# Differential attention on one core: the second softmax's factor in an accumulating form and a tile later, the head norm's statistics on GpSimd

## The chip, the core and the metric

The kernel runs on one core of a Trainium2 chip. The metric is the time of one execution on the device, in microseconds (us). A core has five engines that run side by side and meet at semaphores: TensorE (PE in the rows; its weight loads are PEld), VectorE (DVE), ScalarE (ACT), GpSimd (POOL) and SyncE (SP), which issues the DMAs here. Each engine takes its instructions in the order of its own queue. SBUF is the working memory, PSUM is where TensorE writes.

## What is computed

The program is a two-layer trunk over 1024 latent tokens and 256 context tokens, width 1024. The change lies in the mixer of the second layer, differential attention with 8 heads. Each head has two softmaxes over all 1280 keys, and the second is subtracted with a weight `lam`:

```python
def diff_attn_core(q, k, v, lam):
    s = jnp.einsum('bqhcd,bkhcd->bhcqk', q, k) * DIFF_HEAD_DIM ** -0.5
    p = jax.nn.softmax(s, axis=-1)
    w = p[:, :, 0] - lam * p[:, :, 1]
    return jnp.einsum('bhqk,bkhe->bqhe', w, v)

def finish(o):                       # o: (b, l, 8 heads, 128)
    o = rms_norm(o, subln_gain) * (1.0 - lam_init)
    return o.reshape(b, l, D_MODEL) @ w_out
```

`rms_norm` divides each row of 128 by the root of its mean square plus EPS. A common factor of a row cancels in it, apart from EPS, so the kernel never divides by the first softmax's sum.

## The kernel before

The attention stage works in 16 groups, one for each head `h` and half `qg` of the queries (512 rows). A group has four query tiles `j` of 128 rows, and each tile two units, `c` = 0 and 1, one for each softmax: 128 units in all.

A unit (`unit` in `qk_units`) writes the scores of 128 queries against 1280 keys to PSUM by TensorE (`sc` 1024 wide, `ct` 256 wide). VectorE copies them to SBUF negated and takes the row minimum on the way, with an accumulator output (L1017 and L1018, in the rows TENSOR_SCALAR_CACHE_REDUCE, each followed by a short DVE_READ_ACCUMULATOR). ScalarE takes the exponential and the row sum (L1019). After the second unit of a tile the two exponentials are combined: VectorE forms the factor -lam * sum0 / sum1, 128 rows by 1 column, with a reciprocal (L1022) and a `scalar_tensor_tensor` (L1023); then e1 is multiplied by it, on GpSimd for `j` in `POOLM` = (1, 2, 3) (L1029) and on ScalarE for `j` = 0 (L1031); then GpSimd adds it to e0 (L1032). In the very first group two tiles are combined by VectorE alone (`RAMP`, L1025).

The main loop goes over the groups and over ten blocks `kt` of 128 keys. For each block TensorE transposes the four combined tiles (L1187), ScalarE and VectorE split the result in a high and a low part (`split`, L55 and L56, tile `wt`), and TensorE multiplies with the values in three passes (L1191 to L1193, into `po`). `advance` keeps the units up to five ahead of the next group, so the scores of later groups are made in between. There are 2 PSUM buffers for `sc`, 3 buffers for e1 and 11 for e0.

After a group `post` runs: ScalarE copies `po` out, TensorE transposes it back (L1051), VectorE copies it (L1053), ScalarE sums squares (L1056), VectorE squares the sums of the first softmax for the EPS term (L1059). Once a head has both halves, `norm` adds the two terms (L1067) and takes an inverse root by three Newton steps in `rsqrt_ops` (L60, L62, and three times L65, L67, L69): twelve VectorE instructions on 128 rows by 8 columns for a head. GpSimd multiplies with the result (L1071). For the last head `norm` runs for each half by itself, and the multiplication is VectorE's.

Each engine's order is fixed when the program is built.

Of the kernel before, what the change touches and what calls it, by code (L numbers as in the profile page):

```python
# [13 lines left out]
I32 = mybir.dt.int32  # L14
AF = mybir.ActivationFunctionType
ALU = mybir.AluOpType
# [4 lines left out]
P = 128  # L21
# [4 lines left out]
T = L + LC  # L26
# [4 lines left out]
EPS = 1e-6  # L31
LAM_INIT = 0.8 - 0.6 * math.exp(-0.3)
# [3 lines left out]
def trunk(tc, a, dbg=None, stop=99):  # L36
    nc = tc.nc
    V, S, G, PE = nc.vector, nc.scalar, nc.gpsimd, nc.tensor
# [7 lines left out]
    def r32(ap):  # L46
        return ap.bitcast(F32)
# [10 lines left out]
    def rsqrt_ops(y, v, t, steps=3):  # L58
        yi = y.bitcast(I32)
        V.tensor_scalar(yi, v.bitcast(I32), 1, None, op0=ALU.logical_shift_right)  # L60
        yield
        V.tensor_scalar(yi, yi, -1, 0x5F3759DF, op0=ALU.mult, op1=ALU.add)  # L62
        yield
        for _ in range(steps):
            V.tensor_tensor(out=t, in0=y, in1=y, op=ALU.mult)  # L65
            yield
            V.scalar_tensor_tensor(out=t, in0=t, scalar=-0.5, in1=v, op0=ALU.mult, op1=ALU.mult)  # L67
            yield
            V.scalar_tensor_tensor(out=y, in0=t, scalar=1.5, in1=y, op0=ALU.add, op1=ALU.mult)  # L69
            yield  # L70

    def run(*gens):

        gens = list(gens)
        while gens:
            for g in list(gens):
                try:
                    next(g)
                except StopIteration:
                    gens.remove(g)  # L80

    def rsqrt(y, v, t):
        run(rsqrt_ops(y, v, t))
# [3 lines left out]
    def later(n, fn):  # L87
        pend.append([n, fn])
# [85 lines left out]
    for n, i in enumerate(PAIRS):  # L174
# [4 lines left out]
        if n % 2:  # L179
            j = n // 2  # L180
# [21 lines left out]
    subln = vec[:, 152:153]  # L202
# [234 lines left out]
    for dq in range(4):  # L437
        for i in range(2):
# [5 lines left out]
                                   op0=ALU.mult, op1=ALU.subtract)  # L444
# [406 lines left out]
    for j in range(2):  # L851
        for s in range(2):
            for cc in range(2):
                V.tensor_tensor(out=tabs[:, j, s, :, cc * HD:(cc + 1) * HD], in0=rope[s],
                                in1=gns[:, j, cc * HD:(cc + 1) * HD].unsqueeze(1).broadcast_to([P, 8, HD]), op=ALU.mult)
# [62 lines left out]
    def load_k(h):  # L918
        heads[h] = [[kq.tile([P, T], F32R, name=f"k{c}") for c in range(2)]]
        for c in range(2):  # L920
            nc.sync.dma_start(r32(heads[h][0][c]), kD[2 * h + c])
# [25 lines left out]
    op = up3.enter_context(tc.tile_pool(name="op", bufs=1, reuse_waits="tile"))  # L947
# [24 lines left out]
    nlam = cst.tile([P, 1], F32, name="nlam")  # L972
    V.tensor_tensor(out=nlam, in0=ls[:, 3:4], in1=ls[:, 2:3], op=ALU.subtract)
    V.tensor_scalar(nlam, nlam, -LAM_INIT, None, op0=ALU.add)
    sg = cst.tile([P, 1], F32, name="sg")
    V.tensor_scalar(sg, subln, 1.0 - LAM_INIT, None, op0=ALU.mult)

    oT = {}
    pairs = {}
    NE, LEAD, POOLM, RAMP = (11, 3), 5, (1, 2, 3), (1, 3)  # L980

    def load_v(h):
        vs = ap.tile([P, 2, 10, P], F32R, name="v")
        for s in range(2):
            nc.sync.dma_start(r32(vs[:, s]), vD[s, :, h * P:(h + 1) * P].rearrange("(t p) e -> p t e", p=P))
        heads[h].append(vs)

    def qk_units(h, qg):

        if (h, qg) not in queries:  # L990
            if qg == 0:
                load_k(h)
            load_q(h, qg)
        if qg == 0:
            load_v(h)
        ks, qs = heads[h][0], queries[h, qg]
        st = ap.tile([P, 16, 4], F32, name="st", bufs=6)
        wts = [None] * 4
        es_ = {}
        ct = {}  # L1000

        def scores(out, c, jsl, ksl):
            PE.matmul(out, qs[:, c, 0, jsl], ks[c][:, ksl], start=True, stop=False)
            PE.matmul(out, qs[:, c, 1, jsl], ks[c][:, ksl], start=False, stop=True)  # L1004

        def unit(j, c):
            jsl = slice(j * P, (j + 1) * P)
            col = lambda i: st[:, i, j:j + 1]
            sc = pss.tile([P, 2, 512], F32, name="sc")
            for bk in range(2):  # L1010
                scores(sc[:, bk], c, jsl, slice(bk * 512, (bk + 1) * 512))
            if c == 0:
                ct[j] = pst.tile([P, 2, LC], F32, name="ct", bufs=1)
                for cc in range(2):
                    scores(ct[j][:, cc], cc, jsl, slice(L, T))
            e = ap.tile([P, T], F32, name=f"e{c}", bufs=NE[c])
            V.tensor_scalar(e[:, 0:L], sc.rearrange("p a b -> p (a b)"), -1.0, 3.0e38, op0=ALU.mult, op1=ALU.min, accum_out=col(c))  # L1017
            V.tensor_scalar(e[:, L:T], ct[j][:, c], -1.0, col(c), op0=ALU.mult, op1=ALU.min, accum_out=col(4 + c))  # L1018
            S.activation(out=e, in_=e, func=AF.Exp, scale=-1.0, bias=col(4 + c), accum_out=col(10 + c))  # L1019
            es_[c] = e  # L1020
            if c == 1:
                V.reciprocal(col(12), col(11))  # L1022
                V.scalar_tensor_tensor(out=col(12), in0=col(12), scalar=nlam, in1=col(10), op0=ALU.mult, op1=ALU.mult)  # L1023
                if (h, qg) == (0, 0) and j in RAMP:
                    V.scalar_tensor_tensor(out=es_[0], in0=es_[1], scalar=col(12), in1=es_[0], op0=ALU.mult, op1=ALU.add)  # L1025
                    wts[j] = es_[0]
                    return
                if j in POOLM:
                    G.tensor_tensor(out=es_[1], in0=es_[1], in1=col(12).broadcast_to([P, T]), op=ALU.mult)  # L1029
                else:  # L1030
                    S.activation(out=es_[1], in_=es_[1], func=AF.Copy, scale=col(12))  # L1031
                G.tensor_tensor(out=es_[0], in0=es_[0], in1=es_[1], op=ALU.add)  # L1032
                wts[j] = es_[0]

        return [lambda j=j, c=c: unit(j, c) for j in range(4) for c in range(2)], st, wts

# [2 lines left out]
    def post(h, qg, po, st):  # L1039

        both = h < H - 1
        if qg == 0:
            posts[h] = (ap.tile([P, 4, 8], F32, name="sn"), {})
        sn, ons = posts[h]
        of = ap.tile([P, 512], F32, name="of", bufs=1)
        S.activation(out=of, in_=po, func=AF.Copy)

        def p1():
            pt = pst.tile([P, 512], F32, name="pt")
            for j in range(4):  # L1050
                PE.transpose(out=pt[:, j * P:(j + 1) * P], in_=of[:, j * P:(j + 1) * P], identity=ident)  # L1051
            on = ap.tile([P, 512], F32, name="on", bufs=2)
            V.tensor_copy(on, pt)  # L1053
            for j in range(4):
                jk = ap.tile([P, P], BF16, name="jk")
                S.activation(out=jk, in_=pt[:, j * P:(j + 1) * P], func=AF.Square, accum_out=sn[:, 0, 4 * qg + j:4 * qg + j + 1])  # L1056
            ons[qg] = on
            z = sn[:, 1, 4 * qg:4 * qg + 4]
            V.scalar_tensor_tensor(out=z, in0=st[:, 10], scalar=EPS, in1=st[:, 10], op0=ALU.mult, op1=ALU.mult)  # L1059
            if not both:  # L1060
                norm((qg,))
            elif qg:
                later(1, lambda: norm((0, 1)))

        def norm(qs):
            s0, s1, s2_, s3 = (sn[:, i, 4 * qs[0]:4 * qs[-1] + 4] for i in range(4))
            V.scalar_tensor_tensor(out=s0, in0=s0, scalar=1.0 / P, in1=s1, op0=ALU.mult, op1=ALU.add)  # L1067
            rsqrt(s2_, s0, s3)
            for q in qs:
                on = ons[q]  # L1070
                (G if both else V).tensor_tensor(out=on.rearrange("p (j d) -> p j d", j=4), in0=on.rearrange("p (j d) -> p j d", j=4),  # L1071
                                                 in1=sn[:, 2, 4 * q:4 * q + 4].unsqueeze(2).broadcast_to([P, 4, P]), op=ALU.mult)
                later(6 + 2 * q if both else 2, lambda q=q, on=on: p2(q, on))

        def p2(q, on):
            pt = pst.tile([P, 512], F32, name="pt")
            for j in range(4):
                PE.transpose(out=pt[:, j * P:(j + 1) * P], in_=on[:, j * P:(j + 1) * P], identity=ident)
            if h % 2 == 0:
                pairs[q] = ot(h + q, F32)  # L1080
            oT[q, h] = pairs[q][:, h % 2]
            S.activation(out=oT[q, h], in_=pt, func=AF.Copy, scale=sg)

        later(2 if both else 1, p1)
# [14 lines left out]
    def advance(target):  # L1099
        nonlocal done  # L1100
        while done < target:
            if not stream:
                n = len(info)
                if n >= len(groups):
                    return
                need(n)
            stream.pop(0)()
            done += 1
# [68 lines left out]
    op0 = oproj0()  # L1177
    L0, LS = 3, 5
    advance(8 + L0)
    for gi, (h, qg) in enumerate(groups):  # L1180
        st, wts = info[gi]
# [376 lines left out]
    out = a["out"].rearrange("o t d -> (o t) d")  # L1558
# [124 lines left out]
```

## Time and profile before

| | us |
|---|---|
| median of 3 runs | 2795.05 (2791.34 to 2796.46) |
| the profiled execution | 2793.9 |
| its span, first to last instruction | 2792.1 |
| stretch of the 128 attention units in it, 1538.6 to 1948.0 | 409.4 |

The page of the profile gives the busy time of each engine over the span. A stretch of it is read from the busy times of that window, the instructions grouped by line, and the instructions in order of time. A group of instructions has a count, a busy time and a mean; one line gives the shortest, median and longest of them.

### The profile page before, as it was taken

What the parts mean: (1) busy time and instruction counts of PE and PEld (TensorE: products, weight loads), DVE (VectorE), ACT (ScalarE), POOL (GpSimd) and SP (SyncE); (2) the same over time, 40 slices, a digit from 0 to 9 for tenths busy, and PEclk for the clock granted to TensorE, in tenths of its full rate; (3) what the DMA queues carried; (4) which work ended last, traced back from release to release, by engine and by line L of the source; (5) the groups of instructions that cost most, each with busy time, mean ns of one, the idle gap of its engine ahead of it and who ended that gap; (6) DMA issues with size and microseconds to landing.
All of it is one profiled execution on the core that took longest, in us unless ns stands there. A gap on an engine that the chain in (4) does not pass through costs nothing.

```text
span 2792.1 us, 35671 instructions
## 1 busy us (share of the span) xinstructions
PE 2664.8 (95%) x13234; PEld 2182.4 (78%) x13234; DVE 1609.0 (58%) x2920; ACT 1106.5 (40%) x1940; POOL 960.1 (34%) x648
## 2 busy tenths in 40 slices
PE   6999999999999999999999888898987999999999
PEld 4678888888888888878888666676766788888887
DVE  7744644434333434586764999999666555555342
ACT  5642333222322111333343776687434333334231
POOL 4431024221211000013351676777046666651000
PEclk9999999999999999999999999999999999999999
DMA  6682122222222111143335523222243222226352
GB/s 210 203 272 84 31 76 80 84 87 79 88 83 68 39 38 38 50 138 116 114 114 185 157 83 107 83 69 84 80 128 94 87 87 82 82 79 208 109 181 87
DMA packets 284480, 290.64 MB, mean 104 GB/s; under 512 B 16249, under 2 KB 201874, under 8 KB 284306
## 3 DMA queue, kind: packets, MB, share of 16 engines
q1 hardware_dynamic: 282146, 284.69, 32.8%
q0 software_dynamic: 2160, 3.67, 0.4%
q8 instruction: 104, 1.70, 0.3%
q14 instruction: 70, 0.57, 0.1%
HBM read 234.83 MB, written 53.48 MB: 103 GB/s over the span
## 4 chain that ended last, share of the span: by engine, by line
PE 71%; DVE 11%; issue 8%; POOL 6%; DMA 2%; ACT 2%; SPq 0%; POOLq 0%; DVEq 0%; ACTq 0%
PE ps L50 12%; PE ps L52 12%; PE ps L51 12%; PE b L1418 4%; PE b L1416 4%; PE b L1417 4%; PE b L51 3%; PE b L52 3%; PE b L50 3%; DVE e L1017 2%; POOL xn L894 2%; POOL t L895 2%; PE pt L1187 1%; PE ps L229 1%; DVE wt L56 1%
## 5 line engine op out<-in xcount | busy, mean ns | idle before, releaser
L50 PE MATMUL ps<-un,whl 128*128 128x512 f32 x1184 | 464.4, 393 | 1.4 <-ACT XT L592 1.2
L51 PE MATMUL ps<-un,whl 128*128 128x512 f32 x1184 | 461.3, 390 | 0.0
L52 PE MATMUL ps<-un,whl 128*128 128x512 f32 x1184 | 460.9, 389 | 0.0
L56 DVE TENSOR_TENSOR whl<-raw,whl 128x512 fp32r<-128x512 f32 x219 | 170.8, 793 | 271.2 <-ACT whl L55 270.5
L50 PEld LDWEIGHTS ps<-un,whl 128*128 128x128 f32 x1184 | 222.4, 188 | 54.9 <-issue 3.5
L52 PEld LDWEIGHTS ps<-un,whl 128*128 128x128 f32 x1184 | 222.3, 188 | 46.9
L51 PEld LDWEIGHTS ps<-un,whl 128*128 128x128 f32 x1184 | 222.6, 188 | 44.8 <-issue 0.7
L55 ACT ACTIVATE whl<-raw 128x512 fp32r<-128x512 f32 x219 | 134.7, 628 | 246.2 <-PE ps L52 178.1
L736 DVE SCALAR_TENSOR_TENSOR XT<-ps,mods,XT 128x512 f32<-128x512 f32 (+1 forms) x264 | 170.3, 660 | 85.2 <-PE ps L52 84.9
L262 POOL TENSOR_TENSOR acc<-acc,aw 128x512 f32<-128x512 f32 x84 | 112.6, 1340 | 296.4 <-ACT acc L258 231.2
L1032 POOL TENSOR_TENSOR e<-e,e 128x1280 f32<-128x1280 f32 x62 | 182.9, 2951 | 91.3 <-DMA q<-qD 52.8
L1019 ACT ACTIVATE e<-e,st 128x1280 f32<-128x1280 f32 x128 | 174.7, 1366 | 62.0 <-DVE e L1018 45.7
L607 POOL TENSOR_TENSOR nacc<-nacc,s 128x512 f32<-128x512 f32 (+1 forms) x35 | 41.0, 1172 | 414.2 <-ACT s L606 392.7
L51 PE MATMUL ps<-u,whl 128*128 128x256 f32 x592 | 167.5, 283 | 0.0
L52 PE MATMUL ps<-u,whl 128*128 128x256 f32 x592 | 167.4, 283 | 0.0
L50 PE MATMUL ps<-u,whl 128*128 128x256 f32 x592 | 167.3, 283 | 0.0
L1017 DVE TENSOR_SCALAR_CACHE_REDUCE e<-sc 128x1024 f32<-128x1024 f32 x128 | 154.8, 1216 | 10.3 <-PE sc L1004 8.1
L819 PE MATMUL ps<-whl,un 128*128 128x512 f32 x384 | 152.9, 398 | 0.0
L820 PE MATMUL ps<-whl,un 128*128 128x512 f32 x384 | 150.2, 392 | 1.0 <-DVE whl L56 0.9
L821 PE MATMUL ps<-whl,un 128*128 128x512 f32 x384 | 149.9, 391 | 0.0
L51 PE MATMUL b<-au,wu 128*128 128x512 f32 x336 | 130.9, 390 | 0.1
L50 PE MATMUL b<-au,wu 128*128 128x512 f32 x336 | 130.8, 390 | 0.0
(419 smaller groups left out, 6436.3 us busy)
## 6 DMA issues: line engine op xcount, KB each, us to landing
aw<-in_w_ada SPq DMA_DIRECT2D x96, 256.0 KB, 2.8
raw<-in_ffn_w_in SPq DMA_DIRECT2D x88, 256.0 KB, 2.9
wr<-in_ffn_w_out SPq DMA_DIRECT2D x42, 512.0 KB, 4.1
wada<-in_w_ada SPq DMA_DIRECT2D x48, 256.0 KB, 3.3
un<-in_w_ada SPq DMA_DIRECT2D x48, 256.0 KB, 4.5
raw<-in_diff_w_in SPq DMA_DIRECT2D x48, 256.0 KB, 3.5
rq<-in_ffn_w_in SPq DMA_DIRECT2D x24, 512.0 KB, 5.6
raw<-in_ffn_w_out SPq DMA_DIRECT2D x44, 256.0 KB, 2.9
```

Of the source, the lines that this page charges most:

```text
L50: PE.matmul(out, wh, mh, start=start, stop=False)
L51: PE.matmul(out, wh, ml, start=False, stop=False)
L52: PE.matmul(out, wl, mh, start=False, stop=stop)
L55: S.activation(out=hl[:, 0], in_=src, func=AF.Copy)
L56: (lo_eng or V).tensor_tensor(out=hl[:, 1], in0=src, in1=r32(hl[:, 0]), op=ALU.subtract)
L736: V.scalar_tensor_tensor(out=xs, in0=pt, scalar=gmod[c][:, nn:nn + 1], in1=xs, op0=ALU.mult, op1=ALU.add)
L819: PE.matmul(pt, hk[:, 0, tsl], ws[k][:, 0], start=k == 0, stop=False)
L820: PE.matmul(pt, hk[:, 0, tsl], ws[k][:, 1], start=False, stop=False)
L821: PE.matmul(pt, hk[:, 1, tsl], ws[k][:, 0], start=False, stop=k == NC - 1)
L1017: V.tensor_scalar(e[:, 0:L], sc.rearrange("p a b -> p (a b)"), -1.0, 3.0e38, op0=ALU.mult, op1=ALU.min, accum_out=col(c))
L1019: S.activation(out=e, in_=e, func=AF.Exp, scale=-1.0, bias=col(4 + c), accum_out=col(10 + c))
L1032: G.tensor_tensor(out=es_[0], in0=es_[0], in1=es_[1], op=ALU.add)
```

## The change

The factor's second step becomes a `tensor_scalar` with two column operands and an accumulator output, whose one-column sum is the factor; the multiplication and addition of a tile are written out after the next unit's exponential, through the list `comb`; `POOLM` becomes (0, 2), so GpSimd and ScalarE multiply in turn (14 of the 46 multiplications by GpSimd go to ScalarE); and the EPS term, the sum of the terms and the inverse root go to GpSimd, in a form that GpSimd has (`rsqrt_pool`, 14 instructions), except the inverse root of the last head's second half. The mean's 1/128 moves into the constants.

```diff
+    def rsqrt_pool(y, v, t, steps=3):
+        G.tensor_scalar(y.bitcast(I32), v.bitcast(I32), -0.5, float(0x5F3759DF), op0=ALU.mult, op1=ALU.add)
+        G.tensor_scalar(v, v, -0.5, None, op0=ALU.mult)
+        for _ in range(steps):
+            G.tensor_tensor(out=t, in0=y, in1=y, op=ALU.mult)
+            G.tensor_tensor(out=t, in0=t, in1=v, op=ALU.mult)
+            G.tensor_scalar(t, t, 1.5, None, op0=ALU.add)
+            G.tensor_tensor(out=y, in0=y, in1=t, op=ALU.mult)
...
-    V.tensor_scalar(sg, subln, 1.0 - LAM_INIT, None, op0=ALU.mult)
+    V.tensor_scalar(sg, subln, (1.0 - LAM_INIT) * math.sqrt(P), None, op0=ALU.mult)
...
-    NE, LEAD, POOLM, RAMP = (11, 3), 5, (1, 2, 3), (1, 3)
+    NE, LEAD, POOLM, RAMP = (11, 3), 5, (0, 2), (1, 3)
...
+            while comb:
+                comb.pop()()
             if c == 1:
-                V.reciprocal(col(12), col(11))
-                V.scalar_tensor_tensor(out=col(12), in0=col(12), scalar=nlam, in1=col(10), op0=ALU.mult, op1=ALU.mult)
...
+                e0, e1 = es_[0], es_[1]
+                wts[j] = e0
+                comb.append(lambda: combine(j, col, e0, e1))
+
+        def combine(j, col, e0, e1):
+
+            V.reciprocal(col(12), col(11))
+            V.tensor_scalar(col(13), col(12), col(10), nlam, op0=ALU.mult, op1=ALU.mult, accum_out=col(14))
...
+            if j in POOLM:
+                G.tensor_tensor(out=e1, in0=e1, in1=col(14).broadcast_to([P, T]), op=ALU.mult)
+            else:
+                S.activation(out=e1, in_=e1, func=AF.Copy, scale=col(14))
+            G.tensor_tensor(out=e0, in0=e0, in1=e1, op=ALU.add)
...
-            V.scalar_tensor_tensor(out=z, in0=st[:, 10], scalar=EPS, in1=st[:, 10], op0=ALU.mult, op1=ALU.mult)
+            G.tensor_tensor(out=z, in0=st[:, 10], in1=st[:, 10], op=ALU.mult)
...
-            V.scalar_tensor_tensor(out=s0, in0=s0, scalar=1.0 / P, in1=s1, op0=ALU.mult, op1=ALU.add)
-            rsqrt(s2_, s0, s3)
+            G.tensor_scalar(s1, s1, P * EPS, None, op0=ALU.mult)
+            G.tensor_tensor(out=s0, in0=s0, in1=s1, op=ALU.add)
+            (rsqrt if qs == (1,) else rsqrt_pool)(s2_, s0, s3)
```

How the queues change is seen at two places. On VectorE, in the third group, this stood before around two tiles' factors (names as in the code; a number after a name tells buffers apart):

```order
L1018 TENSOR_SCALAR e_13290,st<-ct,st 128x256
L56 TENSOR_TENSOR wt<-pt,wt 128x512
L1017 TENSOR_SCALAR e_13319,st<-sc 128x1024
L1022 RECIPROCAL st<-st 128x1
L1017 TENSOR_SCALAR e_13339,st<-sc 128x1024
L1023 SCALAR_TENSOR_TENSOR st<-st,nlam 128x1
L1018 TENSOR_SCALAR e_13319,st<-ct,st 128x256
```

and this stands there now (L1029 and L1030 are the unit's two copies, L1042 and L1043 the factor, in the changed file's numbering):

```order
L1030 TENSOR_SCALAR e_13290,st<-ct,st 128x256
L56 TENSOR_TENSOR wt<-pt,wt 128x512
L1029 TENSOR_SCALAR e_13315,st<-sc 128x1024
L1029 TENSOR_SCALAR e_13339,st<-sc 128x1024
L1030 TENSOR_SCALAR e_13315,st<-ct,st 128x256
L1042 RECIPROCAL st<-st 128x1
L56 TENSOR_TENSOR wt<-pt,wt 128x512
L1043 TENSOR_SCALAR st<-st,nlam 128x1
```

The factor of a tile has moved behind the next unit's copies, and its second step has changed its form.

On GpSimd, in the fourth group, where the first head's norm falls, this stood before:

```order
L1032 TENSOR_TENSOR e_13554<-e_13554,e_13574 128x1280
L1029 TENSOR_TENSOR e_13637<-e_13637,st 128x1280
L1032 TENSOR_TENSOR e_13603<-e_13603,e_13637 128x1280
L1029 TENSOR_TENSOR e_13704<-e_13704,st 128x1280
L1032 TENSOR_TENSOR e_13667<-e_13667,e_13704 128x1280
L1071 TENSOR_TENSOR on<-on,sn 128x512 x2
```

and now this (L1048 is the multiplication, L1051 the addition, L1077 to L1086 the statistics, L74 to L80 the inverse root):

```order
L1051 TENSOR_TENSOR e_13550<-e_13550,e_13574 128x1280
L1048 TENSOR_TENSOR e_13637<-e_13637,st 128x1280
L1077 TENSOR_TENSOR sn<-st 128x4
L1051 TENSOR_TENSOR e_13599<-e_13599,e_13637 128x1280
L1085 TENSOR_SCALAR sn<-sn 128x8
L1086 TENSOR_TENSOR sn<-sn 128x8
L74 TENSOR_SCALAR sn<-sn 128x8
L75 TENSOR_SCALAR sn<-sn 128x8
L77 TENSOR_TENSOR sn<-sn 128x8
L78 TENSOR_TENSOR sn<-sn 128x8
L79 TENSOR_SCALAR sn<-sn 128x8
L80 TENSOR_TENSOR sn<-sn 128x8
```

The norm's small instructions (eight more of the last four lines' kind follow) stand between the additions of the third and of the fourth tile of the group, and the fourth tile's multiplication has left this queue.

## Rows read from the trace of the kernel before

**Rows 1.** The page's busy us, share of the span and instructions of each engine.
```profile
PE 2664.8 (95%) x13234; PEld 2182.4 (78%) x13234; DVE 1609.0 (58%) x2920; ACT 1106.5 (40%) x1940; POOL 960.1 (34%) x648
```
**Rows 2.** Busy times by stretch: all units; eight with a norm; eight without one.
```profile
core 0: us, PE busy (x) PEld busy (x) DVE busy (x) ACT busy (x) POOL busy (x), PEclk, DMA share, GB/s
1538.60:1948.00 409.40, 357.56 (x1872) 279.42 (x1872) 388.70 (x887) 302.91 (x557) 295.43 (x118) 0.97 0.34 97
1621.00:1653.20 32.20, 25.18 (x129) 19.29 (x127) 30.40 (x64) 21.83 (x42) 22.46 (x11) 0.95 0.40 114
1653.20:1675.80 22.60, 21.92 (x121) 17.28 (x121) 20.88 (x52) 18.34 (x40) 17.50 (x7) 1.00 0.20 54
```
**Rows 3.** VectorE by line from 1538 to 1948: count, busy us and mean ns, idle before.
```profile
L56 DVE TENSOR_TENSOR wt<-pt,wt 128x512 fp32r<-128x512 f32 x142 | 95.4, 683 | 2.7 <-ACT wt L55 2.3
...
L1023 DVE SCALAR_TENSOR_TENSOR st<-st,nlam 128x1 f32<-128x1 f32 x63 | 37.1, 589 | 0.1
...
L1067 DVE SCALAR_TENSOR_TENSOR sn<-sn 128x8 f32<-128x8 f32 x6 | 8.1, 1358 | 0.2 <-ACT jk L1056 0.2
...
L67 DVE SCALAR_TENSOR_TENSOR sn<-sn 128x8 f32<-128x8 f32 x18 | 6.4, 354 | 0.0
```
**Rows 4.** All units' stretch: busy us (instructions) on the norm's tile sn alone.
```profile
core 0: us, DVE busy (x) POOL busy (x), PEclk, DMA share, GB/s
1538.60:1948.00 409.40, 54.91 (x87) 12.25 (x12) 0.97 0.34 97
```
**Rows 5.** Single lines: ns of the shortest, median and longest instruction; first, last start.
```profile
L1023 DVE SCALAR_TENSOR_TENSOR st<-st,nlam x64: 200/215/2800, 1545.3 to 1952.1; 128x1 f32<-128x1 f32 x64
L69 DVE SCALAR_TENSOR_TENSOR sn<-sn x27: 150/159/2492, 1628.3 to 2008.5; 128x8 f32<-128x8 f32 x21, 128x4 f32<-128x4 f32 x6
L1022 DVE RECIPROCAL st<-st x64: 145/156/165, 1544.8 to 1951.9; 128x1 f32<-128x1 f32 x64
L1018 DVE TENSOR_SCALAR_CACHE_REDUCE e<-ct,st x128: 457/474/485, 1540.0 to 1949.6; 128x256 f32<-128x256 f32 x128
L1018 DVE DVE_READ_ACCUMULATOR e<-ct,st x128: 74/82/89, 1540.4 to 1950.0; 128x1 f32 x128
```
**Rows 6.** GpSimd in order of time, 1556.5 to 1561: start us, length us, instruction.
```profile
1554.63 2.32 POOL L1029 TENSOR_TENSOR e<-e,st 128x1280 f32<-128x1280 f32 x1 [4.03 <-DVE st L1023]
1557.03 2.88 POOL L1032 TENSOR_TENSOR e<-e,e 128x1280 f32<-128x1280 f32 x1
```
**Rows 7.** VectorE in order of time, the same stretch.
```profile
1557.13 2.80 DVE L1023 SCALAR_TENSOR_TENSOR st<-st,nlam 128x1 f32<-128x1 f32 x1
```
**Rows 8.** GpSimd by line and shape over the span.
```profile
L1029 POOL TENSOR_TENSOR e<-e,st 128x1280 f32<-128x1280 f32 x46 | 107.3, 2332 | 49.8 <-DVE st L1023 26.7 <-DVE sn L67 6.6 <-DVE sn L65 6.0
...
L607 POOL TENSOR_TENSOR nacc<-nacc,s 128x512 f32<-128x512 f32 x21 | 29.1, 1384 | 73.6 <-ACT s L606 53.0 <-ACT nacc L603 19.4
...
L607 POOL TENSOR_TENSOR nacc<-nacc,s 128x256 f32<-128x256 f32 x14 | 11.9, 854 | 340.6 <-ACT s L606 339.7
...
L489 POOL COPY un<-gp 128x2 f32<-128x2 f32 x8 | 2.0, 249 | 39.0 <-ACT gp L483 39.0
```
**Rows 9.** ScalarE's multiplication, by line from 1540 to 1960.
```profile
L1031 ACT ACTIVATE e<-e,st 128x1280 f32<-128x1280 f32 x16 | 21.8, 1361 | 12.3 <-DVE sn L67 8.0 <-DVE st L1023 3.7 <-DVE sn L69 0.5
```
**Rows 10.** TensorE in order of time, 1657 to 1662.
```profile
1659.25 0.39 PE L1193 MATMUL po<-wt,v 128*128 128x512 f32 x1
1659.48 1.03 PE L1187 MATMUL pt<-ident,e 128*128 128x128 f32 x8
1660.27 0.36 PE L1003 MATMUL ct<-k,q 128*128 128x256 f32 x1
1660.47 0.28 PE L1004 MATMUL ct<-k,q 128*128 128x256 f32 x1
1660.59 0.28 PE L1003 MATMUL ct<-k,q 128*128 128x256 f32 x1
```

More of the change, by code (lines that the diff above doesn't have):

```diff
@@ L986, in load_v @@
         heads[h].append(vs)
+    comb = []
     def qk_units(h, qg):
@@ L1020, in unit @@
             es_[c] = e
+            while comb:
+                comb.pop()()
             if c == 1:
-                V.reciprocal(col(12), col(11))
-                V.scalar_tensor_tensor(out=col(12), in0=col(12), scalar=nlam, in1=col(10), op0=ALU.mult, op1=ALU.mult)
[L1024 to L1033, printed above, removed]
+                e0, e1 = es_[0], es_[1]
[4 more added lines that the diff above has]
+            V.tensor_scalar(col(13), col(12), col(10), nlam, op0=ALU.mult, op1=ALU.mult, accum_out=col(14))
+            if (h, qg) == (0, 0) and j in RAMP:
+                V.scalar_tensor_tensor(out=e0, in0=e1, scalar=col(14), in1=e0, op0=ALU.mult, op1=ALU.add)
+                return
+            if j in POOLM:
[3 more added lines that the diff above has]
+            G.tensor_tensor(out=e0, in0=e0, in1=e1, op=ALU.add)
         return [lambda j=j, c=c: unit(j, c) for j in range(4) for c in range(2)], st, wts
@@ L1104, in advance @@
                 if n >= len(groups):
+                    while comb:
+                        comb.pop()()
                     return
```

## The prediction

> **What bounds the kernel now.** Over the whole span TensorE looks like the bound, with 95% against VectorE's 58% [rows 1], but that is a mean over stages. The change touches the stretch of the 128 attention units alone, so I read that stretch first. There VectorE is busy 388.7 of 409.4 us, 95%; TensorE 357.6, ScalarE 302.9, GpSimd 295.4 [rows 2]. So VectorE sets the pace of this stage. Outside it nothing is edited.
>
> Next come VectorE's instructions by line [rows 3]. The factor's second step, L1023, works on one column and takes 589 ns in the mean, 37.1 us for 63. The seven lines of the norm (L1059, L1067, L60, L62, L65, L67, L69) work on 4 or 8 columns and take 54.9 us for 87 [rows 4], 0.63 each, with line means from 354 to 1358 ns [rows 3]. That is 92 us in 150 instructions. They are not slow by nature: L1023 has a median of 215 ns and a longest of 2800, L69 a median of 159 and a longest of 2492 [rows 5]. What they do in the long ones is seen in order of time: an L1023 starts at 1557.13 and ends at 1559.93 [rows 7], while GpSimd runs an addition from 1557.03 to 1559.91 [rows 6]. The small VectorE instruction sits through the GpSimd instruction and ends with it. If all of L1023 took the median, 63 x 0.215 = 13.5 us would stand where 37.1 stand, so this line loses 23.6 us that way. At some 0.17 us each, the norm's lines would be 87 x 0.17 = 15 us and not 54.9; they lose 40. The loss is some 64 us in all, on the engine that sets the end.
>
> The two neighbouring stretches of eight units show what it is worth: the eight with a norm chain take 32.2 us, the eight after them, nearly without one, 22.6 us [rows 2]. In the first TensorE is busy 25.2 of 32.2 us, at a mean granted clock of 0.95; in the second 21.9 of 22.6, at 1.00, which is the 2.4 GHz level.
>
> **The change part by part.**
>
> The factor's form. 64 `scalar_tensor_tensor` go, 64 accumulating `tensor_scalar` come, each with an accumulator read. The trace has this form only with PSUM sources: L1018 spreads from 457 to 485 ns over 128 instructions [rows 5] while GpSimd is busy 72% of the stretch, so it never sits through anything. The new one reads SBUF columns. The nearest row of that kind is the reciprocal, one SBUF column, 145 to 165 ns in all 64 [rows 5], which doesn't wait either. I take 0.215 for the instruction and 0.08 for the read, 0.30 us: 63 x 0.30 = 19 us where 37.1 stand. If it waits as L1023 does, nothing is gained here and 64 x 0.08 = 5 us are lost; if it costs no more than the reciprocal, it is 10 us.
>
> On this the Trainium skill has a rule ("SBUF — State Buffer", section "Who interferes with whom"): a VectorE instruction with two SBUF inputs, or in a two-port mode, contends with GpSimd and one of the two waits for the other's end, and the `tensor_scalar` form that writes out its accumulator has no two-port mode. The trace agrees for PSUM sources (457 to 485 ns); no run here shows it for SBUF columns. By this rule the 23.6 us go, without it they stay.
>
> The norm. Its seven lines leave VectorE, 54.9 us [rows 4]. With the factor that is 388.7 - 37.1 - 54.9 + 19 = 316 us of VectorE work left.
>
> GpSimd. 14 of the multiplications leave: 14 x 2.332 = 32.6 us [rows 8], so 295.4 - 32.6 = 263 us stay. What comes are 15 squarings and, for seven heads, 16 instructions of 8 columns, 127 in the stretch, the seventh head's at its edge. No row has that size on this engine with two inputs. From above: 854 ns at 256 columns; from below: a copy of 2 columns, 249 ns [rows 8]. The line through 1384 ns at 512 and 854 at 256 has 2.07 ns a column and gives 0.34 us at 8, near the lower row, which is also the nearest in size. Each waits for the one before it; the addition behind its own multiplication started 1557.03 - 1556.95 = 0.08 us after its end [rows 6]. So 0.42 us each, 127 x 0.42 = 53, together 316 us (bounds 0.25 and 0.85: 295 and 371). The additions behind a burst of 16 come some 7 us later; the fourth tile's addition is the one behind it. Its transposes are due only when the units are five ahead, some 5 x 22.6 / 8 = 14 us, so it is late for nobody as long as GpSimd isn't behind already. The burst begins with a wait for ScalarE's sum of squares; the same addition is queued behind that too, out of the same 14 us.
>
> On such moves the Trainium skill speaks against the change ("GPSIMD Engine Reference", section 4.1): elementwise work belongs on VectorE, since GpSimd is about twice as slow with two inputs. The trace agrees on the ratio, 0.34 estimated against VectorE's 0.16 us undisturbed. By the rule alone the move would cost, 127 x 0.18 = 23 us; but VectorE is not undisturbed here, and its mean for the removed lines is 54.9 / 87 = 0.63 us.
>
> ScalarE. 14 multiplications come, 14 x 1.361 = 19 us [rows 9]: 322 us.
>
> TensorE is unchanged. Its busy time has tails in it, so I count steps between starts: 0.23 us for 512 columns (1659.25 to 1659.48), 0.12 for 256, 0.79 for eight transposes, and some 0.09 more for the first matmul behind transposes [rows 10]. 128 units of four wide and two narrow score matmuls, 512 x 0.23 + 256 x 0.12, 142 blocks [rows 3] x (3 x 0.23 + 0.4 + 0.09) of transposes and values, and 26 x 0.48 for the transposes of `post` make 118 + 31 + 168 + 12 = 329 us. No matmul goes and no DMA moves.
>
> The later combination. The factor no longer waits for the exponential just issued, and a tile is ready one unit (some 2.8 us) later, out of the 14 us above. e1 has three buffers, so the third tile from here waits for the addition: six units, 17 us, against one unit, 2.8, a multiplication and an addition, 5.2 [rows 6], and a ScalarE pass of that size, 1.4 [rows 9]. I cost this at nothing; the cover is those 7 us, and it is gone when a burst meets a late tile.
>
> So four engines stand at 316, 316, 322 and 329 us where one stood at 389. None can run without a gap. The best measure of the new pace is the quiet stretch: eight units in 22.6 us with TensorE at 97% and VectorE at 92%. 128 units at that pace are 361.6 us, 47.8 less than 409.4. I take off 2 us for accumulator reads and for bursts. The gain is 46 us: span 2746, and with the 1.8 us by which the profiled execution (2793.9) exceeded its span, 2748. The profiled execution lies 1.1 us under the median, which I neglect. The tail behind the last unit keeps its work; there the first half's norm of the last head goes to GpSimd, 16 x 0.42 = 7 us of chain where stalled VectorE instructions stood, and VectorE's multiplication waits for it with the splits behind it: a few us either way.
>
> **The rivals.**
>
> GpSimd or the hand-overs are tighter than thought. A small instruction at 0.65 us makes 263 + 83 = 346 us of GpSimd, and at nine tenths use 384: gain 25, 2769. Against it speaks the copy of 249 ns, for it the chain in which each instruction waits for the last. With e1's buffers running out as well, up to 2787.
>
> The accumulating form stalls like the old one. Then VectorE keeps 24 us of its 64 and the gain falls to about 22: 2772. The reciprocal speaks against it.
>
> GpSimd becomes the bound and the kernel slower. At a use of 0.9, GpSimd sets the old pace when its work reaches 409.4 x 0.9 = 368 us, that is (368 - 263) / 127 = 0.83 us for a small instruction. The row of 256 columns costs just that, 854 ns; if the cost is one of starting and not of columns, or the conversion to integers is slow, at 1.0 us it is 390 / 0.9 = 433, 24 us more: 2818.
>
> TensorE alone sets the pace, at 97% of its steps: 329 / 0.97 = 339, gain 70, 2724.
>
> **How the numbers follow.** The forecast, a gain between 30 and 62 us, has 0.57. TensorE alone 0.07. GpSimd or hand-overs with a small gain 0.16, the stalling form 0.06, a new loss that eats the gain to within 0.2% 0.05, slower 0.09. So faster 0.86, same 0.05, slower 0.09. 0.2%, 5.6 us, is about what a measurement of this kernel can tell from no change. The range leaves out the most of TensorE alone below and the last two cases above: 2724 to 2785.
>
> **What would show it.** Right: the new factor at 0.2 to 0.3 us with no long ones; small GpSimd instructions at 0.3 to 0.45 us; VectorE's busy share of the stretch near 87% and TensorE's over 93%; groups with a norm as fast as those without. Wrong: GpSimd over 95% in the stretch, transposes that wait for GpSimd's addition, VectorE's copies that wait for an e1 buffer. The prediction fails first if the small GpSimd instructions cost 0.8 us or more.

## The result and the profile after

The changed kernel takes 2758.2 us (median of 4 runs, 2756.6 to 2763.2) against 2795.8 for the kernel before beside it: ratio 0.9872, 95% interval 0.986 to 0.9884, a gain of 37.6 us. The forecast was 2748, from a gain of 46; the range of 2724 to 2785 holds the result. Two of its numbers have to be looked at apart: what the stretch of the units gave, and what stood outside it.

Row 1 of the page after (busy us, share of the span, instructions), beside [rows 1]:

```profile
PE 2657.3 (96%) x13234; PEld 2185.1 (79%) x13234; DVE 1540.8 (56%) x2871; ACT 1119.2 (41%) x1954; POOL 961.0 (35%) x780
```

VectorE has lost 68 us of busy time; GpSimd has 132 instructions more and as much busy time as before. Now the stretch, beside [rows 2]: all units; one group of eight units in its middle; its last six groups.

```profile
core 0: us, PE busy (x) PEld busy (x) DVE busy (x) ACT busy (x) POOL busy (x), PEclk, DMA share, GB/s
1542.30:1904.50 362.20, 339.50 (x1853) 273.50 (x1854) 320.00 (x861) 311.64 (x558) 283.47 (x217) 0.98 0.36 106
1670.80:1700.70 29.90, 25.90 (x132) 20.74 (x130) 21.24 (x57) 20.43 (x39) 26.68 (x27) 0.89 0.42 118
1772.40:1904.50 132.10, 130.12 (x739) 107.03 (x738) 122.07 (x328) 123.42 (x225) 112.43 (x97) 1.00 0.33 94
```

The 409.4 us of [rows 2] end a little too early: the second copy of the last unit ends at 1950.1 (its accumulator read starts at 1950.0, [rows 5]), and the 362.2 of now run to the end of that copy. Measured to the same point, the kernel before has

```profile
1538.60:1950.10 411.50, 357.56 (x1872) 279.42 (x1872) 390.80 (x890) 302.91 (x557) 296.51 (x118) 0.97 0.34 97
```

So the 128 units take 49.3 us less, where the forecast for this stretch was 361.6 us, 47.8 less, of which 2 were taken off for accumulator reads and bursts. In its last six groups a group takes 132.1 / 6 = 22.0 us, a little better than the quiet 22.6 of before, and no longer with every second group slow. The group in the middle is not like that: 29.9 us, with the granted clock at 0.89 and GpSimd busy for 26.7. It holds a norm, and so do three of the last six groups: the sign "groups with a norm as fast as those without" came true at the end of the stretch and failed in its middle.

Of the 49.3 us the profiled executions keep 35.4 (span 2756.7 against 2792.1). The stretch begins 3.7 us later, before any instruction that was moved; its first copy starts between 1538.6 and 1545.1 in the 14 profiles of this study, and at 1538.6 and 1542.0 in two kernels that are alike up to there, so this is put down to spread between executions. What lies behind the stretch is 10.2 us longer (852.2 against 842.0).

Next, the two groups of instructions on which the forecast rested. The factor in its new form, with its read (ns of the shortest, median and longest; beside L1023 in [rows 5]):

```profile
L1043 DVE TENSOR_SCALAR_CACHE_REDUCE st<-st,nlam x64: 261/269/277, 1549.0 to 1911.1; 128x1 f32<-128x1 f32 x64
L1043 DVE DVE_READ_ACCUMULATOR st<-st,nlam x64: 77/83/90, 1549.2 to 1911.3; 128x1 f32 x64
```

Not one of 64 is long. With the read it is 0.35 us, 22 us in all where 37.1 stood. The norm's tile `sn` in the stretch, beside [rows 4]:

```profile
core 0: us, DVE busy (x) POOL busy (x), PEclk, DMA share, GB/s
1542.30:1904.50 362.20, 0.00 (x0) 36.03 (x125) 0.98 0.36 106
```

and two of its lines on GpSimd:

```profile
L77 POOL TENSOR_TENSOR sn<-sn x24: 197/201/205, 1627.8 to 1936.2; 128x8 f32<-128x8 f32 x21, 128x4 f32<-128x4 f32 x3
L79 POOL TENSOR_SCALAR sn<-sn x24: 222/233/697, 1628.3 to 1936.8; 128x8 f32<-128x8 f32 x21, 128x4 f32<-128x4 f32 x3
```

VectorE has nothing left of the norm in the stretch. GpSimd's 36.0 us include its multiplications of before, 12.25 us in [rows 4], so 24 us for the 113 small instructions in it, 0.21 each.

Last, five waits of the units and their transposes in the stretch (who waited for whom; us in all, times, longest):

```profile
POOL e L1051 <- ACT e L1050: 29.1, 18, 6.2
ACT e L1031 <- DVE e L1030: 23.0, 26, 3.9
PEld sc L1015 <- DVE e L1029: 20.7, 26, 4.0
DVE e L1029 <- POOL e L1051: 14.6, 9, 4.4
...
PEld pt L1208 <- POOL e L1051: 6.8, 2, 3.6
```

L1029 and L1030 are the unit's two copies, L1050 is ScalarE's multiplication, L1051 GpSimd's addition. The fourth row is a copy that waits for an e1 buffer: a sign that the prediction named for a wrong step. It is the subject of half of the experiments. The fifth row is another of these signs, a transpose that waits for GpSimd's addition. The third, GpSimd over 95% busy, did not come: 283.5 of 362.2 us are 78%.

### The profile page after: what moved, and what is told of

Same layout as the page of the kernel before. It is cut to its first block, busy times and chain, and to the rows that moved or that the text cites. A ratio compares the mean times of both kernels' runs of the same rounds, so it can differ in the third digit from the quotient of the medians.

```text
span 2756.7 us, 35769 instructions
## 1 busy us (share of the span) xinstructions
PE 2657.3 (96%) x13234; PEld 2185.1 (79%) x13234; DVE 1540.8 (56%) x2871; ACT 1119.2 (41%) x1954; POOL 961.0 (35%) x780
## 5 line engine op out<-in xcount | busy, mean ns | idle before, releaser
L1051 POOL TENSOR_TENSOR e<-e,e 128x1280 f32<-128x1280 f32 x62 | 183.0, 2955 | 31.3 <-ACT e L1050 29.1
L1029 DVE TENSOR_SCALAR_CACHE_REDUCE e<-sc 128x1024 f32<-128x1024 f32 x128 | 155.2, 1218 | 28.1 <-POOL e L1051 14.6
```

The source lines that it names most:

```text
L1051: G.tensor_tensor(out=e0, in0=e0, in1=e1, op=ALU.add)
```

## Experiments

Each ratio is to the kernel before on the same chip; its medians lie between 2795.4 and 2796.5, so that times of different runs can be set side by side to about 1 us.

### The form and the norm, each alone and each undone

**The form alone**, in the kernel before:

```diff
-V.scalar_tensor_tensor(out=col(12), in0=col(12), scalar=nlam, in1=col(10), op0=ALU.mult, op1=ALU.mult)
+V.tensor_scalar(col(13), col(12), col(10), nlam, op0=ALU.mult, op1=ALU.mult, accum_out=col(14))
```

(and col(14) read where col(12) was).

> The kernel before with one edit, the factor's second step in the accumulating form. Theory (VectorE sets the pace with its work and its stalls, the norm's stalls among them): some 24 us of stall go and 5 us of accumulator reads come, but the groups with a norm keep theirs, and freed time there meets waits for GpSimd: faster than before by 5 to 18 us (2777 to 2790). Rival (each stall taken away is worth its whole length): faster by 19 us or more. Second rival (only the norm counts): within 3 us of 2795.

Measured: 2781.4, ratio 0.9949 (0.9934 to 0.9964), 15 us faster, as the theory had it.

**The form undone**, in the changed kernel: the same edit backwards.

> The changed kernel with the factor's second step as scalar_tensor_tensor again, all else as changed. My theory (VectorE's small instructions sat through GpSimd's long ones, and that set the pace): the 64 factors again have long instructions, some 20 to 24 us of VectorE in all; VectorE now has slack beside TensorE, so part of it is hidden: slower than the changed kernel by 5 to 18 us (2763 to 2776). Rival (the gain is GpSimd's lighter load and the later place of the combination, not the form): within 3 us of 2758.

Measured: 2775.3, 0.9932 (0.9916 to 0.9948), 17 us slower than the changed kernel, as the theory had it. Its factor:

```profile
L1043 DVE SCALAR_TENSOR_TENSOR st<-st,nlam x64: 205/236/2452, 1545.8 to 1926.9; 128x1 f32<-128x1 f32 x64
```

The old form is the quicker one where nothing disturbs it (205 ns against 261) and has the long ones back. 15 and 17 us from two sides: the form is worth nearly the 18 that the sum put.

**Both edits, without the other two**, in the kernel before: the form as above, and the norm's statistics on GpSimd; `POOLM` stays (1, 2, 3), and a tile is combined at once.

```diff
-V.scalar_tensor_tensor(out=s0, in0=s0, scalar=1.0 / P, in1=s1, op0=ALU.mult, op1=ALU.add)
-rsqrt(s2_, s0, s3)
+G.tensor_scalar(s1, s1, P * EPS, None, op0=ALU.mult)
+G.tensor_tensor(out=s0, in0=s0, in1=s1, op=ALU.add)
+(rsqrt if qs == (1,) else rsqrt_pool)(s2_, s0, s3)
```

(with the squaring and the constants as in the change)

> The kernel before with the two form edits, the accumulating factor and the norm's statistics and inverse root on GpSimd, without the new split of the multiplications and without the later combination. VectorE has the changed kernel's work. GpSimd has 46 multiplications and the small instructions, some 330 us. Theory (parts work together: the pace is set where GpSimd's burst delays an addition that VectorE waits for): 2770 to 2785, short of the changed kernel by 12 to 27 us. Rival (VectorE's work alone counts): within 4 us of 2758.

Measured: 2748.9, 0.9831 (0.9815 to 0.9847): 47.6 us faster than before, and 9.3 faster than the whole change. That was expected of no theory as written: the two edits give the gain that was forecast for the whole, and the other two take some of it away. The stretch of its units (columns as above):

```profile
1545.10:1898.60 353.50, 337.39 (x1862) 271.21 (x1863) 322.85 (x863) 298.18 (x547) 313.66 (x230) 1.00 0.38 109
```

and two of its waits there:

```profile
POOL e L1042 <- ACT e L1041: 8.5, 5, 5.8
...
DVE e L1027 <- POOL e L1042: 5.8, 5, 1.8
```

353.5 us with the clock at 1.00; the waits of the addition for ScalarE's multiplication are 8.5 us where the changed kernel has 29.1, and those of the copies for an e1 buffer 5.8 where it has 14.6. GpSimd is busier than in the changed kernel (313.7 against 283.5 us) and does no harm.

**The norm undone**, in the changed kernel: the last diff backwards.

> The changed kernel with the norm's statistics and the inverse root on VectorE again. My theory: some 87 small VectorE instructions sit through GpSimd again, about 40 us of waiting and 15 of work, while GpSimd is relieved of some 128 x 0.29 = 37 us: slower by 12 to 30 us (2770 to 2788). Rival (the statistics are a burden on GpSimd, which delays the additions, and the gain comes from elsewhere): the same or faster, 2750 to 2758.

Measured: 2793.0, 0.9996 (0.9986 to 1.0006): 35 us slower than the changed kernel, nearly all of the gain, and more than either theory had. VectorE and GpSimd on the norm's tile in the stretch:

```profile
1541.10:1942.50 401.40, 60.68 (x87) 12.24 (x12) 0.95 0.33 97
```

one of its lines:

```profile
L67 DVE SCALAR_TENSOR_TENSOR sn<-sn x27: 153/163/2747, 1630.9 to 2008.2; 128x8 f32<-128x8 f32 x21, 128x4 f32<-128x4 f32 x6
```

and two waits:

```profile
POOL e L1051 <- ACT e L1050: 62.7, 25, 5.0
ACT e L1031 <- DVE e L1030: 52.5, 29, 5.5
```

The same 87 instructions cost VectorE 60.7 us, with a median of 163 ns on this line and a longest of 2747. A late VectorE passes on through ScalarE (52.5 us of waits for the copies, 23.0 in the changed kernel) to GpSimd (62.7, where there are 29.1).

Set side by side, these four and the two ends give the steps:

| step | us |
|---|---|
| before to form alone | -15.1 |
| form alone to form and norm | -32.5 |
| form and norm to the whole change (split and later place) | +9.3 |
| the same last step without the norm's move (form alone to norm undone) | +11.6 |

So the form gives 15, the norm 32 to 35 (what it loses behind the stretch is in this), and the new split of the multiplications together with the later place costs 9 to 12 in either setting.

### The split and the later place

**The split undone**, in the changed kernel:

```diff
-POOLM, RAMP = (0, 2), (1, 3)
+POOLM, RAMP = (1, 2, 3), (1, 3)
```

> The changed kernel with three of four multiplications on GpSimd again. My theory: GpSimd gets 14 x 2.33 = 33 us more and ScalarE 19 less; GpSimd goes from some 290 to 323 of 362 us, so the additions come late more often: slower by 4 to 15 us (2762 to 2773). Rival (the new balance between GpSimd and ScalarE is the gain): slower by 25 us or more. Third possibility (ScalarE was the tighter one): faster.

Measured: 2760.4, 0.9879 (0.9864 to 0.9893): no difference to the changed kernel, where 4 to 15 us of loss were expected. GpSimd has room for the third multiplication.

**The later place undone**, in the changed kernel:

```diff
-                comb.append(lambda: combine(j, col, e0, e1))
+                combine(j, col, e0, e1)
```

> The changed kernel with the combination written out at once, right behind the tile's second exponential, and not behind the next unit's. My theory: VectorE then waits for the exponential at the reciprocal as it did before (3.6 us in all) and the additions come a unit earlier: within 6 us either way (2752 to 2764). Rival (the later place is what keeps VectorE and ScalarE from waiting for each other): slower by 12 us or more.

Measured: 2774.9, 0.9929 (0.9914 to 0.9943): 16.7 us slower than the changed kernel. The theory that the place is worth nothing fell, the rival's number held. Waits in the stretch:

```profile
POOL e L1051 <- ACT e L1050: 42.9, 20, 6.2
PEld sc L1015 <- DVE e L1029: 34.9, 33, 3.0
POOL e L1048 <- DVE st L1043: 32.2, 14, 4.1
...
DVE e L1029 <- POOL e L1051: 20.7, 8, 3.1
```

All four are larger than in the changed kernel (the third is 12.7 us there). With the split (0, 2), where every second tile goes from VectorE over ScalarE to GpSimd, the later place gains 16.7 us; with (1, 2, 3) it costs 11.5, since that split is the 2748.9 above at once and 2760.4 later. The split, in turn, costs 26 us at once and nothing later. So neither of the two edits has a price of its own.

### A fourth e1 buffer

The copies that wait for the addition point to e1's three buffers. A fourth one takes away what makes them wait and moves no instruction to another engine:

```diff
-    NE, LEAD, POOLM, RAMP = (11, 3), 5, ...
+    NE, LEAD, POOLM, RAMP = (11, 4), 5, ...
```

In the changed kernel:

> The changed kernel with four buffers for e1 and not three. Theory (where VectorE waits for an addition, 14.6 us in all, it waits for the e1 buffer that the addition reads): these waits go, and TensorE, which is otherwise the bound, takes up the time only in the groups that had them: faster by 3 to 10 us (2748 to 2755). Rival (TensorE is the bound all through and the waits cost nothing): within 2 us of 2758.

Measured: 2740.8, 0.9807 (0.9793 to 0.9822): 17.4 us faster than the changed kernel, where the theory had at most 10 and the rival 2. The stretch:

```profile
1541.00:1888.60 347.60, 335.13 (x1854) 271.17 (x1855) 319.62 (x861) 311.29 (x559) 283.44 (x217) 0.99 0.38 110
```

and waits in it:

```profile
POOL e L1051 <- ACT e L1050: 21.9, 16, 3.9
ACT e L1031 <- DVE e L1030: 17.6, 22, 3.9
...
PEld sc L1015 <- DVE e L1029: 10.7, 20, 1.2
```

No copy waits for the addition any more in this trace, and the score matmuls wait for the copies for half as long. The same busy times stand in 347.6 us instead of 362.2.

In the kernel with the later place undone:

> The changed kernel with the combination written out at once, which gave 2774.9, and four buffers for e1. Theory (what the later place is worth is that e1 buffers are free in time behind GpSimd's bursts; VectorE waited 20.7 us for additions there): 2755 to 2763. Rival (the later place is worth its 17 us by the order of VectorE's and ScalarE's queues, not by buffers): 2771 to 2777.

Measured: 2754.6, 0.9856 (0.9841 to 0.987): 20 us faster than without the buffer, just past the theory's 2755; the rival fell.

In the kernel with form and norm alone:

> The kernel before with the two form edits (2748.9) and four buffers for e1. Theory (there VectorE hardly waits for e1 buffers, so a fourth has little to free, and GpSimd's 46 multiplications stay): 2743 to 2749. Rival (the fourth buffer frees GpSimd's and VectorE's coupling as in the changed kernel, 17 us): 2730 to 2736.

Measured: 2742.7, 0.9809 (0.9794 to 0.9824): 6.2 us faster than without it, at the lower edge of the theory.

The medians, all with the form and the norm's move:

| split and place | three e1 buffers | four |
|---|---|---|
| (1, 2, 3), at once | 2748.9 | 2742.7 |
| (0, 2), later (the change) | 2758.2 | 2740.8 |
| (0, 2), at once | 2774.9 | 2754.6 |
| (1, 2, 3), later | 2760.4 | not run |

With four buffers the change's split and place cost nothing against those of before (2740.8 and 2742.7, intervals that overlap); with three they cost 9.3. So the cost of the two together is one of e1's buffers. In the third row 12 to 14 us remain that a fourth buffer doesn't take away. Its waits with four buffers:

```profile
POOL e L1048 <- DVE st L1043: 28.8, 14, 4.1
POOL e L1051 <- ACT e L1050: 28.7, 15, 4.3
```

and those of the first row with four (L1042 is the addition there, L1041 ScalarE's multiplication, L1039 GpSimd's, L1033 the factor):

```profile
POOL e L1042 <- ACT e L1041: 7.6, 3, 6.0
...
POOL e L1039 <- DVE st L1033: 4.9, 8, 1.0
```

GpSimd stands still for the factor and for ScalarE far longer in the third row. Whether that is the cause or a consequence of another delay was not told apart.

### TensorE's work

**One pass of the values left out** (that with their low part; 160 wide matmuls in all, 160 x 0.23 = 37 us of TensorE steps), in the changed kernel:

```diff
-            PE.matmul(po, vs[:, 1, kt], wt[:, 0], start=False, stop=False)
```

> The changed kernel without the second of the three passes of the product with the values (the low half of the values is left out): 160 matmuls of 0.23 us, 37 us of TensorE less, nothing else. Theory (VectorE no longer sets the pace, TensorE does in the later groups at 95% of its steps): faster than the changed kernel by 14 to 28 us (2730 to 2744); not the whole 37, since VectorE, ScalarE and GpSimd stand close behind. Rival (TensorE is not the bound, the hand-overs are): by 3 to 9 us, what the tail gives (2749 to 2755).

Measured: 2751.8, 0.9844 (0.9829 to 0.9859): 6.4 us faster than the changed kernel, where 14 to 28 were expected if TensorE sets the pace, and 3 to 9 by the rival. The theory fell. The stretch:

```profile
1540.60:1900.40 359.80, 321.01 (x1707) 250.31 (x1707) 318.09 (x858) 308.24 (x554) 281.02 (x216) 0.97 0.36 106
```

and a wait in it:

```profile
PEld sc L1015 <- DVE e L1029: 35.5, 41, 4.0
```

With some 146 matmuls fewer, 34 us of steps, the stretch takes 359.8 us instead of 362.2. TensorE mostly waits longer for the copies (35.5 against 20.7). Its mean clock is 0.97 instead of 0.98; whether that gives back a part of what was taken out was not told apart.

**The same pass left out before:**

> The kernel before without the second of the three passes of the product with the values (the low half of the values is left out), 37 us of TensorE less. Theory (VectorE sets the pace of its 128 units): faster than before by 3 to 10 us, mostly in the last two groups where VectorE has no units (2786 to 2793). Rival (TensorE already shared the bound): by 14 us or more (2782 or less).

Measured: 2798.1, 1.0004 (0.9995 to 1.0014): nothing, where 3 to 10 us were expected. In the profile this is made of two parts, the stretch and what follows up to the last head's last transposes; the third row is that second part in the kernel before:

```profile
1542.00:1945.60 403.60, 337.50 (x1710) 256.61 (x1711) 387.05 (x884) 296.99 (x543) 290.75 (x117) 0.95 0.34 95
1945.60:2014.50 68.90, 57.67 (x266) 43.53 (x265) 49.16 (x98) 35.15 (x81) 13.41 (x6) 0.89 0.29 87
```

```profile
1950.10:2009.90 59.80, 55.13 (x264) 42.87 (x264) 42.37 (x92) 29.89 (x65) 8.10 (x4) 0.95 0.25 75
```

The stretch is 7.9 us shorter than the 411.5 of before, with VectorE busy for 96% of it: VectorE set its pace, as its 95% said, and most of the 37 us of TensorE work stood beside that. Behind the stretch 9.1 us are lost again, at a mean clock of 0.89 against 0.95. Whether the clock is the cause was not tested.

### The last head's first half

Behind the stretch, VectorE's multiplication for the last head waits for GpSimd's inverse root (start, length, instruction, idle before and what ended it), and the transposes wait for VectorE:

```profile
1937.32 0.69 DVE L1090 TENSOR_TENSOR on<-on,sn 128x512 f32<-128x512 f32 x1 [3.49 <-POOL sn L80]
...
1938.16 1.09 PE L1097 MATMUL pt<-ident,on 128*128 128x128 f32 x4 [3.35 <-DVE on L1090]
```

In the five us around this gap and the five after it the clock is low; the third row cuts out the part from the first of these transposes on:

```profile
1935.00:1940.00 5.00, 1.84 (x7) 1.57 (x8) 1.89 (x3) 0.71 (x2) 1.66 (x8) 0.70 0.00 0
1940.00:1945.00 5.00, 5.00 (x20) 4.31 (x19) 2.67 (x4) 2.84 (x5) 0.00 (x0) 0.61 0.00 0
1938.20:1943.70 5.50, 5.50 (x19) 4.76 (x20) 3.62 (x6) 2.92 (x5) 0.00 (x0) 0.50 0.00 0
```

So the chain on GpSimd costs its gap and then some: 5.5 us at 0.50, the 1.2 GHz level. In the changed kernel with four e1 buffers, which has the same tail, that one inverse root goes back to VectorE:

```diff
-            (rsqrt if qs == (1,) else rsqrt_pool)(s2_, s0, s3)
+            (rsqrt_pool if both else rsqrt)(s2_, s0, s3)
```

> The changed kernel with four buffers for e1 (2740.8) and the last head's first half back on VectorE for its inverse root. Theory (in the tail TensorE waited 3.35 us for VectorE's multiplication, that waited for GpSimd's fourteen small instructions, and then ran some 5 us at half clock): 3 to 6 us come back, 2735 to 2738. Rival (the tail is set by the order of TensorE's queue and these waits are replaced by others): 2739 to 2743.

Measured: 2734.3, 0.9779 (0.9765 to 0.9794): 6.6 us faster than the four buffers alone, a little over the 3 to 6 of the theory, and the fastest kernel of the study, 62 us under the kernel before. The same place in it, in two pieces:

```profile
1920.00:1925.00 5.00, 3.63 (x21) 2.85 (x22) 3.45 (x7) 3.42 (x6) 0.00 (x0) 1.00 0.17 52
1925.00:1930.00 5.00, 5.00 (x26) 4.05 (x25) 3.73 (x6) 2.12 (x4) 0.00 (x0) 1.00 0.34 104
```

The clock stays at 1.00 there.

## Why the prediction was right, and where it was not

**The bound.** Right, and shown. VectorE set the pace of the stretch: taking 37 us out of TensorE moved the whole time by nothing and the stretch by 8, and taking small instructions and their waits from VectorE moved 47.6 us, although GpSimd got more work by it (313.7 us for 295.4). The loss by sitting through GpSimd's instructions is on record from both sides, since each edit undone brings the long ones back (2452 ns, 2747 ns) with the time. Nor was the pair in [rows 6] and [rows 7] an accident: between 1535 and 1960 the trace of the kernel before has 48 VectorE instructions on 1, 4 or 8 columns that last over 0.4 us, and each of them ends within 0.05 us of the end of a GpSimd instruction. "Outside it nothing is edited" was not so: the last head's norm lies behind the stretch.

**The factor's form.** Right. 0.35 us with its read, where 0.30 were put; 15 to 17 us of time for 18 forecast. Of the 64 new ones 35 run wholly inside a GpSimd instruction; of the 64 old ones one did. On this the Trainium skill ("SBUF — State Buffer", section "Who interferes with whom") has the rule that the prediction weighed; the 64 instructions between 261 and 277 ns bear it out for SBUF columns too, which no row of before showed.

**The norm.** Right in kind: VectorE keeps 320.0 us, 316 were put. Of the 55 us that left VectorE, 32 to 35 came out as time; the loss behind the stretch is one part of the difference, the rest was not told apart. The Trainium skill's rule for the other direction ("GPSIMD Engine Reference", section 4.1, elementwise work belongs on VectorE) would have had this move cost time; here it gave the larger part of the gain, because VectorE's instructions on this tile took 0.63 us in the mean and not 0.16. Nor is a ratio of two seen at this size: 0.20 to 0.23 us on GpSimd against some 0.16.

**GpSimd.** Mis-sized to the safe side. A small instruction lasts 0.20 to 0.23 us, and in the chain most start 0.28 to 0.34 us after the one they wait for; 0.42 were put, between 0.25 and 0.85. With 113 of the 127 in the stretch they take 24 us where 53 were put. So GpSimd stands at 283.5 us, not 316, and the rival by which it becomes the bound was far off. ScalarE has 311.6 us for 322.

**The pace.** The quiet stretch was the right yardstick: 361.6 us forecast, 362.2 measured. But that is luck, two errors that cancel. The last six groups go at 22.0 us, and form and norm alone reach 353.5; the middle groups lose what that gains.

**The later combination, "at nothing".** This step failed. The prediction saw the cover, some 7 us on e1's three buffers, and the condition under which it is gone, a burst that meets a late tile, and then put no price on it. The trace after has that case. GpSimd in order of time, and then VectorE:

```profile
1683.96 2.04 POOL L1090 TENSOR_TENSOR on<-on,sn 128x512 f32<-128x512 f32 x2
1685.96 2.33 POOL L1048 TENSOR_TENSOR e<-e,st 128x1280 f32<-128x1280 f32 x1
1688.36 5.77 POOL L1051 TENSOR_TENSOR e<-e,e 128x1280 f32<-128x1280 f32 x2
```

```profile
1691.30 1.23 DVE L1029 TENSOR_SCALAR_CACHE_REDUCE e<-sc 128x1024 f32<-128x1024 f32 x1 [4.38 <-POOL e L1051]
```

The norm's small instructions stood ahead of these, from 1676.0 to 1683.9. Then the norm's last multiplications, a tile's multiplication and the first of two additions stand one behind another; the copy that needs the e1 buffer waits 4.38 us, and the units of the next group with it. With the split of before the later place cost 11.5 us, together with the new split 9.3, and the fourth buffer took 17.4 off. The rival of tighter hand-overs named e1's buffers; this part of it came true beside the forecast, for another reason than the price of a small instruction.

**What is next.** TensorE had the largest of the four sums, 329 us, and is busy for 339.5 of 362.2 us now, but 37 us less of it gave 6.4 in all and 2.4 in the stretch: it is not the bound. Of what holds the changed kernel the runs show e1's buffers, 17.4 us; the rest of the chain from the copy over the exponential and the multiplication to the addition is argued from its waits.

**The tail.** "A few us either way" was a loss. The inverse root's 14 instructions there run from 1932.6 to 1937.3, 4.7 us (16 were put at 7), but TensorE had nothing else to do for 3.35 us of it and ran slowly afterwards; putting that one root back on VectorE gave 6.6 us. It isn't all of the 10.2 us by which the part behind the stretch grew: with the whole norm back on VectorE that part is still 6.8 us longer than before (848.8 against 842.0). Why was not tested.

**The total.** The sum put 45.8 us on the stretch and nothing on the rest. In the profiled executions the stretch gave 49.3, so what the total is short of 46 lies outside it: 10.2 us behind it and 3.7 of spread ahead of it. Inside the stretch the 9.3 us of split and place are hidden by a pace that was put too slow: form and norm alone give 47.6 us with the loss of the tail in it. Open are the 12 to 14 us of the split (0, 2) at once with four buffers, the rest of the tail, and the norm's move without the form, which wasn't run.

## What to carry to other kernels

A small instruction whose longest is ten times its median need not be dear by itself: see in order of time whether the long ones end with another engine's instructions. If they do, as here, count the loss as (mean - median) x count, and try another form or another engine. Where an edit lengthens the way of a tile between engines, count the buffers in units of the stage's pace and price the case in which the cover is gone; one more buffer was worth nearly half as much here as the whole change. Let a chain of small instructions stay on the faster engine where TensorE has nothing else to do than wait for it.

## What the runs showed of the hardware

- A small GpSimd instruction is cheaper than the line through its larger ones: 0.20 us for two inputs of 8 columns, where 854 ns at 256 and 1384 ns at 512 [rows 8] give 0.34.
- A plain `tensor_scalar` on VectorE, with one SBUF input of 8 columns, can also sit through a GpSimd instruction, which the accumulating form on one column did in none of 64, nor the reciprocal in any of 64 (37 of them ran wholly inside a GpSimd instruction). From the kernel with the norm undone, where the long one ends at 1952.6 with a GpSimd addition:

```profile
L60 DVE TENSOR_SCALAR sn<-sn x9: 158/164/2804, 1628.5 to 2005.9; 128x8 int32<-128x8 int32 x7, 128x4 int32<-128x4 int32 x2
```

- After a gap of 3.35 us without matmuls TensorE's granted clock was at 0.50, the 1.2 GHz level, for 5.5 us in which the engine was busy throughout; then wide matmuls started 0.23 us apart again, where they had started 0.43 apart.
